# First pass of attention beside HGRN: two 128-query score tiles share one PSUM tile of two banks

## The chip, the cores and the metric

The kernel runs on one core of a Trainium2 chip. The metric is the time of one execution on the device in microseconds (us). A core has a matrix engine (PE; PEld is its weight load, which runs beside it), a vector engine (DVE), an activation engine (ACT), a general engine (POOL) and a queue engine (SP) that issues most of the transfers. Each of them works through its own instructions in order. Matmuls write to PSUM, which has eight banks, each of 512 float32 columns on 128 partitions.

## What is computed

Two layers of a transformer block over 256 context tokens and 2048 latent tokens. One input projection feeds four groups of heads: RG-LRU, HGRN2, a convolution and differential attention. Their gated outputs are joined, projected and added to the stream. The part that matters here is the softmax of attention, whose denominator the kernel finds in a first pass:

```
def attend(q, keys, vals):
    s = jnp.einsum('bqhd,bkhd->bhqk', q, keys).astype(jnp.float32) * scale
    p = jax.nn.softmax(s, axis=-1)
    ...
    a = (p[:, :, 0] - lam * p[:, :, 1]).astype(vals.dtype)
    return jnp.einsum('bhqk,bkhe->bqhe', a, vals)
```

## The kernel before

The instructions are written in one order, and a scheduler of the tile framework, which simulates the engines, decides at build time in which order each engine gets them. On the chip the order on each engine is then fixed.

A layer has four parts. `half0` projects the first half of the tokens. `half1` projects the second half, and beside it run `hgrn` (the HGRN2 scan) and `passes` (the first pass of attention). `first` runs the first 92 of 148 (second layer: 144) steps of the second pass, `attention`, beside `lrus` (two RG-LRU scans), the convolution's norms, `out_weights` (splitting the output weights on POOL) and, in the first layer, `modulations` for the next one. `second` runs the remaining steps beside the output projection and the two convolutions.

`passes` works on one pair of heads `hp` after the other. For each block of 512 queries and each block of keys (256 for block 0, else 512) it calls `pieces`: 16 tiles of 128 queries, each a matmul (score tile `sa`, L1004), a row maximum on DVE (`nm`, L1005), and an Exp with its row sum on ACT (L1006). There are 448 such tiles in each layer. In the code, key blocks 3 and 4 come first, and blocks 0, 1 and 2 last for the queries of the second half: 32 tiles each, those of block 0 only 256 columns wide. `extremes` then turns maxima and sums into one offset per query, transposes it on PE through another `sa` tile, and stores it (`mzd`, L1143).

The PSUM tiles `sa` come from the pool `psA1`: four buffers of one bank. `psm` (`pm`, HGRN) has three banks and `pj1` (`pj`, projections) has one. When `half1` ends, its pools are given up, and those of `first` take their place: `psB` (`sb`, `po`) five banks, `psA2` one, `pq1` two. So an `sb` of the second pass can't be written before `passes` has given up its banks. Before the first `sb`, SP loads the queries (`qst`, L996), the offsets (L1049) and the keys (`kst`, L986).

In a step of `att_b`, PE makes four score matmuls (`sb`, L1176), ACT takes two Exps of 1024 columns (L1180), DVE combines two halves (L1185), and PE adds the step's values to `po` (L1157), some steps later. The first convolution instruction on DVE (L913) that follows in a layer stands, in both kernels, behind the 93rd combination L1185.

Of the kernel before, what the change touches and what calls it, by code (L numbers as in the profile page):

```python
# [8 lines left out]
F32 = mybir.dt.float32  # L9
# [3 lines left out]
AF = mybir.ActivationFunctionType  # L13
ALU = mybir.AluOpType
AX = mybir.AxisListType
# [3 lines left out]
P = 128  # L19
# [35 lines left out]
BLOCKS = [(0, 256)] + [(256 + 512 * j, 512) for j in range(4)]  # L55
# [42 lines left out]
class _Kern:  # L98
# [1000 lines left out]
                yield  # L1099

    def pieces(self, k, c, q, r):
        for s in range(4):
            for i in range(4):
                j = s * 4 + i
                self.piece(k, BLOCKS[c][1], q, s, i, r[0][:, j, c : c + 1], r[1][:, j, c : c + 1])
            yield

    def extremes(self, l, hp, b, nm, zc):

        nc, ap_ = self.nc, self.pc  # L1110
        n = BLOCKS[b][1]
        N = 4 * (n // P)
        C = 5 if b else 1
        with self.tc.high_priority():
            v = nc.vector
            mz = ap_.tile([P, 2, 16], F32, name="mz", bufs=2)
            tm = ap_.tile([P, 16], F32, name="tm", bufs=2)
            if C > 1:
                ng = ap_.tile([P, 16], F32, name="ng", bufs=2)
                v.tensor_reduce(out=ng[:, :N], in_=nm[:, :N, :], axis=AX.X, op=ALU.min)  # L1120
                v.tensor_tensor(
                    out=nm[:, :N, :], in0=ng[:, :N].unsqueeze(2).to_broadcast([P, N, C]), in1=nm[:, :N, :], op=ALU.subtract
                )
                nc.scalar.activation(out=nm[:, :N, :], in_=nm[:, :N, :], func=AF.Exp)
                v.tensor_tensor(out=zc[:, :N, :], in0=zc[:, :N, :], in1=nm[:, :N, :], op=ALU.mult)
                v.tensor_reduce(out=tm[:, :N], in_=zc[:, :N, :], axis=AX.X, op=ALU.add)
                nc.scalar.activation(out=tm[:, :N], in_=tm[:, :N], func=AF.Ln)
            else:
                ng = nm[:, :, 0]
                nc.scalar.activation(out=tm[:, :N], in_=zc[:, :N, 0], func=AF.Ln)  # L1130
            v.tensor_tensor(out=tm[:, :N], in0=tm[:, :N], in1=ng[:, :N], op=ALU.subtract)
            hi = ap_.tile([P, 16], F32R, name="mhi", bufs=2)
            v.tensor_copy(out=hi[:, :N], in_=tm[:, :N])
            v.tensor_copy(out=mz[:, 0, :N], in_=hi[:, :N].bitcast(F32))
            v.tensor_tensor(out=mz[:, 1, :N], in0=tm[:, :N], in1=hi[:, :N].bitcast(F32), op=ALU.subtract)

            mzd = self.dr.tile([2, N, P], F32, name=f"mzd{l}_{hp}_{b}")
            pt = self.psA.tile([P, 512], F32, name="sa")
            for g in range(2):
                nc.tensor.transpose(pt[:N, g * P : (g + 1) * P], mz[:, g, :N], self.ident)  # L1140
            mt = ap_.tile([16, 2, P], F32R, name="mt")
            v.tensor_copy(out=mt[:N].rearrange("n g p -> n (g p)"), in_=pt[:N, : 2 * P])
            nc.sync.dma_start(out=mzd.rearrange("g n p -> n g p"), in_=mt[:N].bitcast(F32))  # L1143
            self.mzd[hp, b] = mzd
# [521 lines left out]
```

## Time and profile before

| what | value |
|---|---|
| three timed runs | 3856.81, 3852.32, 3845.16 us, median 3852.32 |
| the profiled execution | 3839.82 us |
| its span, first to last instruction | 3838.0 us |
| mean granted TensorE clock | 0.943 of full |
| busy: PE, PEld, DVE, ACT, POOL | 90%, 63%, 69%, 58%, 26% |

The profiled execution is 12.5 us below the median of the timed runs. A busy share is a mean over stages that differ; matmuls are pipelined, and the time of one in the profile is its latency, so that the distance between two starts says what one costs in a row of its kind. PEclk is the granted clock, where 1.00 is 2.4 GHz and 0.50 is 1.2 GHz.

### The profile page before, as it was taken

How to read it: one execution, taken by the hardware profiler on the slowest of the kernel's cores; microseconds unless marked ns; L12 is line 12 of the kernel's file. 1: busy time of each engine (PE TensorE's matmuls, PEld its weight loads, DVE VectorE, ACT ScalarE, POOL GpSimd, SP SyncE). 2: the span in 40 equal slices, each digit the busy share in tenths (PEclk: the TensorE clock that was granted, in tenths of full speed). 3: DMA queues.
4: the chain of work that ended last, by engine and by line, in shares of the span. 5: the costliest groups of instructions: out<-in, count | busy, mean ns of one | idle time of the engine just before them, and what ended most of it. 6: DMA issues, size and time to landing. Idle time of an engine off the chain costs nothing. (4 is left out here: it accounts for less than half of the span.)

```text
span 3838.0 us, 61038 instructions
## 1 busy us (share of the span) xinstructions
PE 3471.8 (90%) x21140; PEld 2426.5 (63%) x21140; DVE 2640.7 (69%) x4287; ACT 2211.1 (58%) x4750; POOL 1011.9 (26%) x1588
## 2 busy tenths in 40 slices
PE   6899898999999879999988899889999997899998
PEld 4668676667778634365666686666676784334466
DVE  5967746777787376697438777467887763768842
ACT  3164644766787468755421646536777874886621
POOL 2412124443452130001114231154534203100010
PEclk9899998998999989999999899889999998899999
DMA  5645446434333663443346545364443237434133
GB/s 217 218 163 162 145 165 171 140 114 125 116 96 101 179 221 111 144 131 109 132 142 202 174 168 170 133 177 136 143 125 104 90 102 202 151 89 162 61 124 107
DMA packets 390444, 549.27 MB, mean 143 GB/s; under 512 B 78376, under 2 KB 232024, under 8 KB 390104
## 3 DMA queue, kind: packets, MB, share of 16 engines
q1 hardware_dynamic: 313320, 438.37, 36.9%
q10 hardware_dynamic: 76816, 107.00, 8.0%
q8 instruction: 168, 2.75, 0.3%
q14 instruction: 140, 1.15, 0.1%
HBM read 349.68 MB, written 195.56 MB: 142 GB/s over the span
## 5 line engine op out<-in xcount | busy, mean ns | idle before, releaser
L1006 ACT ACTIVATE sa<-sa,nm 128x512 f32<-128x512 f32 (+1 forms) x1296 | 795.8, 614 | 492.7 <-DVE nm L1005 476.8
L1005 DVE TENSOR_REDUCE nm<-sa 128x1 f32<-128x512 f32 (+1 forms) x1296 | 787.9, 628 | 353.0 <-PE sa L1004 347.7
L499 PE MATMUL pj<-h,wh 128*128 128x256 f32 (+1 forms) x3712 | 962.1, 346 | 39.5 <-ACT s L557 15.2
L499 PEld LDWEIGHTS pj<-h,wh 128*128 128x128 f32 x3712 | 656.7, 197 | 140.0 <-issue 17.4
L1180 ACT ACTIVATE pb<-sb 128x1024 f32<-128x1024 f32 x584 | 568.9, 1019 | 204.3 <-PE sb L1176 192.3
L499 PE MATMUL pj<-h,wl 128*128 128x256 f32 (+1 forms) x1856 | 635.5, 342 | 2.1 <-DMA wl<-wp 2.1
L1185 DVE SCALAR_TENSOR_TENSOR pb<-pb,lam 128x1024 f32<-128x1024 f32 x292 | 381.2, 1307 | 225.0 <-ACT pb L1180 220.4
L1176 PE MATMUL sb<-qst,kst 98*128 98x512 f32 (+1 forms) x1168 | 402.9, 454 | 58.9 <-ACT pb L1180 46.6
L1176 PEld LDWEIGHTS sb<-qst,kst 98*128 98x128 f32 x1168 | 196.0, 198 | 322.8 <-ACT pb L1180 254.8
L499 PEld LDWEIGHTS pj<-h,wl 128*128 128x128 f32 x1856 | 364.2, 196 | 44.3 <-DMA wl<-wp 2.9
L1004 PE MATMUL sa<-k,q 96*128 96x512 f32 (+1 forms) x896 | 351.8, 433 | 31.6 <-ACT sa L1006 29.5
L913 DVE SCALAR_TENSOR_TENSOR m<-m,cols 128x1280 f32<-128x1280 f32 (+1 forms) x240 | 373.9, 1567 | 5.5 <-ACT m L908 4.9
L1157 PE MATMUL po<-pb,V 128*64 128x512 f32 (+1 forms) x1168 | 327.1, 641 | 11.3 <-DVE pb L1185 10.7
L499 PE MATMUL pj<-hx,wh 128*128 128x512 f32 x896 | 297.9, 405 | 10.9 <-ACT s L557 9.6
L1006 ACT ACTIVATION_READ_ACCUMULATOR sa<-sa,nm 128x1 f32 x1296 | 257.7, 199 | 0.6
L133 POOL TENSOR_SCALAR wh<-w 128x1024 fp32r<-128x1024 f32 x56 | 70.4, 1258 | 627.9 <-PE pj L499 521.6
L1004 PEld LDWEIGHTS sa<-k,q 96*128 96x128 f32 x896 | 161.6, 191 | 99.3 <-ACT sa L1006 59.5
L499 PEld LDWEIGHTS pj<-hx,wh 128*128 128x128 f32 x896 | 168.4, 192 | 49.4 <-ACT s L557 10.4
L148 POOL TENSOR_SCALAR rsq<-rsq 128x8 f32<-128x8 f32 (+2 forms) x45 | 16.2, 360 | 659.3 <-DVE rsq L1221 658.5
L133 POOL TENSOR_SCALAR mq<-Q 64x256 f32<-64x256 f32 x238 | 107.7, 454 | 282.0 <-PE pm L1464 170.6
L1004 PE MATMUL sa<-h,xs 96*128 96x512 f32 (+1 forms) x384 | 155.0, 419 | 28.2 <-ACT sa L1006 27.9
L499 PE MATMUL pj<-hx,wl 128*128 128x512 f32 x448 | 179.7, 401 | 0.0
(287 smaller groups left out, 5592.3 us busy)
## 6 DMA issues: line engine op xcount, KB each, us to landing
w<-in_w_in_dram SPq DMA_DIRECT2D x56, 512.0 KB
wp<-wh SPq DMA_DIRECT2D x56, 512.0 KB
wp<-wl SPq DMA_DIRECT2D x56, 512.0 KB
wh<-wp SPq DMA_DIRECT2D x56, 512.0 KB
wl<-wp SPq DMA_DIRECT2D x56, 512.0 KB
ctab<-in_rope_dram SPq DMA_DIRECT2D x32, 512.0 KB
wmod<-in_w_mod_dram SPq DMA_DIRECT2D x32, 512.0 KB
wo<-wop SPq DMA_DIRECT2D x32, 512.0 KB
```

What stands on the lines that cost most here:

```text
L133: self.nc.gpsimd.tensor_scalar(out=out, in0=in_, scalar1=1.0, scalar2=1.0, op0=ALU.mult, op1=ALU.mult)
L148: gp.tensor_scalar(out=ss, in0=ss, scalar1=scale, scalar2=eps, op0=ALU.mult, op1=ALU.add)
L499: nc.tensor.matmul(ps[:, :n], a[:, k, :], hT[:, part, k, o : o + n], start=(m == 0), stop=(m == 23))
L913: nc.vector.scalar_tensor_tensor(out=acc[:, :W], in0=vb[:, k : k + W], scalar=self.col(l, C_FW + 2 * k + ct), in1=acc[:, :W], op0=ALU.mult ...
L1004: nc.tensor.matmul(ps[:, :kn], qst[s][:96, q * P : (q + 1) * P], kst[:96, s, :], start=True, stop=True)
L1005: nc.vector.tensor_reduce(out=nm, in_=ps[:, :kn], axis=AX.X, op=ALU.max, negate=True)
L1006: nc.scalar.activation(out=ps[:, :kn], in_=ps[:, :kn], func=AF.Exp, bias=nm, accum_out=zc)
L1157: nc.tensor.matmul(po[64 * h : 64 * h + 64, :n], V[:, ki, 64 * h : 64 * h + 64], cbs[h][:, :n], start=(kt == 0), stop=(kt == nk - 1), skip ...
L1176: qk = nc.tensor.matmul(ps[:, m, :n], kst[:98, 2 * h + m, ki * P : (ki + 1) * P], qst[2 * h + m][:98, :n], start=True, stop=True,)
L1180: self.exp = nc.scalar.activation(out=pb[:, h, :, :n], in_=ps[:, :, :n], func=AF.Exp)
L1185: nc.vector.scalar_tensor_tensor(out=pb[:, :, 1, :n], in0=pb[:, :, 1, :n], scalar=self.pr["nlam"], in1=pb[:, :, 0, :n], op0=ALU.mult, op1= ...
```

## The change

`pieces` takes two tiles of queries at a time: one PSUM tile of two banks (two buffers in place of four), two matmuls one after the other, then two maxima, then two Exps. Nothing else changes in what is computed; the number and the shapes of instructions are the same. `extremes` takes the same kind of tile and uses its first bank. `early`, the part of the first pass in `half0`, still uses `piece`.

```
     def pieces(self, k, c, q, r):
+
+        nc, n = self.nc, BLOCKS[c][1]
         for s in range(4):
-            for i in range(4):
+            for i in (0, 2):
+                ps = self.psA.tile([P, 2, 512], F32, name="sa", bufs=2)
                 j = s * 4 + i
-                self.piece(k, BLOCKS[c][1], q, s, i, r[0][:, j, c : c + 1], r[1][:, j, c : c + 1])
+                for h in range(2):
+                    nc.tensor.matmul(
+                        ps[:, h, :n], q[s][:96, (i + h) * P : (i + h + 1) * P], k[:96, s, :], start=True, stop=True
+                    )
+                for h in range(2):
+                    nm = r[0][:, j + h, c : c + 1]
+                    nc.vector.tensor_reduce(out=nm, in_=ps[:, h, :n], axis=AX.X, op=ALU.max, negate=True)
+                for h in range(2):
+                    nc.scalar.activation(
+                        out=ps[:, h, :n], in_=ps[:, h, :n], func=AF.Exp, bias=r[0][:, j + h, c : c + 1],
+                        accum_out=r[1][:, j + h, c : c + 1],
+                    )
             yield
...
-            pt = self.psA.tile([P, 512], F32, name="sa")
+            pt = self.psA.tile([P, 2, 512], F32, name="sa", bufs=2)[:, 0]
```

The scheduler orders the whole program anew. (In the changed kernel the matmul is at L1109, and lines behind L1120 are 14 higher: `sb` L1190, `po` L1171, `mzd` L1157.)

On PE in the middle of the first layer's pass, before the change, a single tile (`sa`) stands between runs of HGRN matmuls (`pm`):

```order
L1004 MATMUL sa<-k_10062,q_9289 128x256
L1369 MATMUL pm<-Vb,kt 64x64 x4
L1383 MATMUL pm<-Sn,Vb 64x128 x2
L1004 MATMUL sa<-k_10062,q_9289 128x256
L1388 MATMUL pm<-Q,Sf 64x128 x2
L1004 MATMUL sa<-k_10062,q_9289 128x256
L1383 MATMUL pm<-Sn,Vb 64x128 x2
```

Now, in the same layer, it is pairs:

```order
L1383 MATMUL pm<-Vb,kt 64x64 x4
L1397 MATMUL pm<-Sn,Vb 64x128 x2
L1402 MATMUL pm<-Q,Sf 64x128 x2
L1397 MATMUL pm<-Sn,Vb 64x128 x2
L1478 MATMUL pm<-mq_5104,mk 32x64 x3
L1109 MATMUL sa<-k_8357,q_8365 128x512 x2
L1478 MATMUL pm<-mq_5104,mk 32x64 x5
```

Counted over the pass, an `sa` matmul is directly followed by a `pm` 191 times in the first layer and 160 times in the second before, 97 and 88 times now.

On PE at the end of the second layer's pass, before, the last score tiles (`q_26792` is the last block of queries) stand among the projections (`pj<-h`); 216 more projection matmuls follow behind them, and the first `sb` stands among those:

```order
L1004 MATMUL sa<-k_27917,q_26792 128x512 x2
L1140 MATMUL sa<-ident,mz 16x128 x2
L499 MATMUL pj<-h_22107,wh 128x256 x2
L499 MATMUL pj<-h_22107,wl 128x256
L499 MATMUL pj<-h_22107,wh 128x256 x2
```

Now the last projection comes first. Behind it follow 100 score tiles (96 in the first layer) together with the RG-LRU's gates (`pj<-m,lw`) and the norms (`pj<-m,ones`):

```order
L499 MATMUL pj<-h_22205,wl 128x256
L1109 MATMUL sa<-k_25378,q_26408 128x512 x4
L1109 MATMUL sa<-k_26771,q_26064 128x256 x8
L833 MATMUL pj<-m,lw 128x512 x2
L1109 MATMUL sa<-k_26771,q_26064 128x256 x4
L833 MATMUL pj<-m,lw 128x512 x2
L1109 MATMUL sa<-k_26771,q_26064 128x256 x2
L833 MATMUL pj<-m,lw 128x1
```

At its end, the pass alone is left, and the second pass begins behind it:

```order
L1109 MATMUL sa<-k_27104,q_26408 128x512 x2
L1109 MATMUL sa<-k_27485,q_26064 128x512 x16
L1109 MATMUL sa<-k_27485,q_26408 128x512 x16
L1154 MATMUL sa<-ident,mz 16x128 x4
L1190 MATMUL sb<-qst,kst_30553 128x512 x14
L1171 MATMUL po<-pb,V_30558 64x512 x2
L1190 MATMUL sb<-qst,kst_30553 128x512 x2
```

In the first layer the 144 matmuls of `modulations` have moved in the same way: before they stood among the second pass, now they all stand among the last score tiles.

On SP at that place in the second layer, before, the stores of the offsets follow weight loads (`wh`, `wl`), and the queries of the second pass follow them:

```order
L483 DMA wh<-wp_7_1_20177 128x1024
L484 DMA wl<-wp_7_1_20177 128x1024
L1143 DMA mzd_1_3_28265<-mt 16x2x128
L1143 DMA mzd_1_4_28334<-mt 16x2x128
L996 DMA qst<-qh_18343 32x512
L996 DMA qst<-ql_18344 32x512
```

Now the loads of the RG-LRU (`m<-...`) and of the output weights (`wo<-`, stored again as `wo<-wop` when POOL has split them) come before these, and the last keys of the pass (`k_27485`) stand between them:

```order
L1509 DMA wo_30703<-wop 128x2x512
L1505 DMA wo<-in_w_out_dram 128x512
L986 DMA k_27485<-kh_18121 32x4x512 x2
L986 DMA k_27485<-kl_18122 32x4x512
L865 DMA m<-g_1_18114 128x1023
```

The queries stand behind the offsets, at the end of these:

```order
L899 DMA m<-lyf_18128 128x1023
L865 DMA m<-g_1_18114 128x1023
L1157 DMA mzd_1_3_27817<-mt 16x2x128
L1157 DMA mzd_1_4_27886<-mt 16x2x128
L996 DMA qst<-qh_18119 32x512
```

What moved: the last fifth of the pass now stands behind the projections, the work that used to accompany the first 92 steps of the second pass stands beside that fifth, and the second pass follows both.

## Rows read from the trace of the kernel before

**Rows 1.** Busy time by stage (window, its length, each engine's us; PEclk, DMA share)

```profile
620.00:1266.00 646.00, 606.79 (x5488) 460.50 (x5488) 502.38 (x1146) 455.24 (x1298) 269.10 (x578) 0.95 0.41 123
1266.00:1313.00 47.00, 36.69 (x270) 33.78 (x270) 3.99 (x15) 5.74 (x13) 1.91 (x5) 0.96 0.76 176
1313.00:1613.00 300.00, 260.74 (x1237) 113.04 (x1238) 199.28 (x219) 230.97 (x266) 58.43 (x51) 0.93 0.50 153
1506.00:1606.00 100.00, 99.34 (x398) 38.50 (x396) 58.30 (x49) 84.76 (x91) 6.01 (x5) 1.00 0.28 74
3162.00:3195.00 33.00, 26.93 (x205) 24.71 (x203) 2.77 (x10) 5.34 (x11) 0.91 (x3) 1.00 0.70 170
3195.00:3482.00 287.00, 253.05 (x937) 105.30 (x938) 186.72 (x161) 231.08 (x261) 55.55 (x47) 0.92 0.44 137
```

**Rows 2.** The Exps of the second pass (L1180, ACT) in three of these windows

```profile
1313.00:1613.00 300.00, 185.80 (x192) 0.93 0.50 153
1506.00:1606.00 100.00, 83.09 (x87) 1.00 0.28 74
3195.00:3482.00 287.00, 187.56 (x192) 0.92 0.44 137
```

**Rows 3.** The combinations of the second pass (L1185, DVE) in two windows

```profile
1313.00:1613.00 300.00, 121.24 (x93) 0.93 0.50 153
3195.00:3482.00 287.00, 124.73 (x93) 0.92 0.44 137
```

**Rows 4.** PE in order of time, in the pass (start us, us, instruction)

```profile
1054.56 0.28 PE L499 MATMUL pj<-h,wl 128*128 128x256 f32 x1
1054.68 0.40 PE L1004 MATMUL sa<-k,q 96*128 96x512 f32 x1
1054.91 0.40 PE L499 MATMUL pj<-h,wh 128*128 128x256 f32 x2
...
1055.59 0.63 PE L1464 MATMUL pm<-mq,mk 128*32 128x64 f32 x26
1056.15 0.50 PE L1004 MATMUL sa<-k,q 96*128 96x512 f32 x1
1056.58 0.42 PE L1464 MATMUL pm<-mq,mk 128*32 128x64 f32 x12
1056.93 0.51 PE L1004 MATMUL sa<-k,q 96*128 96x512 f32 x1
```

**Rows 5.** Longest waits of PE in the first layer's pass, then in the second's

```profile
PE sa L1004 <- ACT sa L1006: 13.0, 25, 1.8
...
PE sa L1004 <- ACT sa L1006: 16.5, 33, 1.3
```

**Rows 6.** Row maxima (DVE) and Exps (ACT) back to back, and the mean narrow maximum

```profile
1262.21 2.49 DVE L1005 TENSOR_REDUCE nm<-sa 128x1 f32<-128x512 f32 x4 [2.33 <-PE sa L1004]
...
1260.61 0.66 ACT L1006 ACTIVATE sa<-sa,nm 128x512 f32<-128x512 f32 x1
1261.18 0.21 ACT L1006 ACTIVATION_READ_ACCUMULATOR sa<-sa,nm 128x1 f32 x1
1261.27 0.67 ACT L1006 ACTIVATE sa<-sa,nm 128x512 f32<-128x512 f32 x1
...
L1005 DVE TENSOR_REDUCE nm<-sa 128x1 f32<-128x256 f32 x32 | 12.9, 421 | 12.0 <-PE sa L1004 11.5
```

**Rows 7.** End of the first layer's pass: last tiles, SP's issues, first `sb`

```profile
1261.78 1.09 PE L1004 MATMUL sa<-k,q 96*128 96x512 f32 x4
...
1266.32 4.92 SPq L1143 DMA_DIRECT2D mzd<-mt  x2
1271.33 0.37 SPq L996 DMA_DIRECT2D qst<-qh  x1
...
1280.21 0.38 SPq L978 DMA_DIRECT2D V<-av  x1
...
1284.96 0.70 PE L1176 MATMUL sb<-qst,kst 98*128 98x512 f32 x2 [0.61 <-DMA V<-av]
```

**Rows 8.** SP's stores of split output weights, two of sixteen, four stores apart

```profile
1326.19 0.38 SPq L1495 DMA_DIRECT2D wo<-wop  x1
...
1339.75 0.38 SPq L1495 DMA_DIRECT2D wo<-wop  x1
```

## Prediction

> **What bounds the kernel now.** I read the busy times by stage first, then PE's instructions in the pass in order of time, then the waits, and last the handover from the pass to the second pass. The windows [rows 1] show different limits. In the first layer's pass (620 to 1266) PE is busy 607 of 646 us, DVE 502 and ACT 455; with starts back to back [rows 4], PE sets the pace there. Then come 47 us (second layer 33) of projections alone: the last score tile starts at 1261.78 [rows 7] and DVE and ACT have next to nothing. Then come the first 92 steps of the second pass, 300 and 287 us, with the RG-LRU, the norms and (first layer) the modulations beside them. There PE is busy 261 of 300 and 253 of 287, ACT 231 and 231, DVE 199 and 187: no engine is full. Once that company is gone (1506 to 1606) PE is at 99.3 of 100 us at a granted clock of 1.00, and 87 Exps go by [rows 1, 2].
>
> **The change part by part.** The numbers of matmuls, maxima and Exps stay, so the time can change only by order and by waits. I sum four parts for each layer (first / second), against the profiled execution of 3839.8 us (span 3838.0).
>
> a) Until the last projection. The order now has 96 / 100 score tiles behind the last projection, where it had none. A score matmul of 512 columns between projections takes 0.23 us to the next start (1054.68 to 1054.91), a projection of 256 takes 0.12 [rows 4]. The first layer moves 64 wide and 32 narrow tiles out: 64 x 0.23 + 32 x 0.12 = 19; the second 68 wide, 32 narrow: 19.5. Second, PE changes between score and HGRN matmuls less often: 191 to 97, and 160 to 88. A score matmul ahead of HGRN matmuls takes 0.43 (1056.15 to 1056.58) in place of 0.23, and the runs of 26 and 12 HGRN matmuls take 0.56 and 0.35 us, which is 0.015 for each and 0.17 for the run [rows 4]. So one change costs about 0.20 + 0.17 = 0.37 us: 94 x 0.37 = 35, 72 x 0.37 = 27. Third, the window of projections alone has 270 and 205 matmuls [rows 1]; at 0.12 that is 32 and 25 us, and it takes 47 and 33. Those projections now have score pairs among them; of these 15 and 8 us I count about half, 8 and 5. Sum 62 / 51. The 0.37 comes from one place, and a pair can make PE wait where a single did not, so I take some 85%: **53 / 43** us earlier. Bounds: the moved tiles alone (19), or all.
>
> b) From the last projection to the last score tile, a new stretch. DVE has the most to do in it. Four wide maxima back to back take 2.49 us, so 0.62 each; a narrow one has a mean of 0.42 [rows 6]. 64 x 0.62 + 32 x 0.42 = 53; second layer 56. The other DVE work that accompanied the 92 steps comes into it: what DVE did there less the combinations, 199 - 121 = 78 and 187 - 125 = 62 [rows 1, 3]. Floor: 131 / 118. (About 9 us of it may stay behind as norms of later heads, so 122 / 109 is the lowest I allow.) ACT has less: Exps start 0.66 us apart (1260.61, 1261.27) [rows 6], so 96 and 100 of them take at most 63 and 66 us, and the other work that it had beside the second pass is 231 - 186 = 45 and 231 - 188 = 43 [rows 1, 2]: 108 / 109. PE's matmuls fit below both. How full DVE gets no row shows, since the maxima depend on matmuls, the Exps on maxima, a PSUM tile comes free only after two Exps, and the gates go to and fro between DVE, ACT, PE and SP. The nearest rows are the same gates beside the old 92 steps, where the busiest engine was filled to 87% and 88% [rows 1]. I take that: 131 / 0.87 = **150**, 118 / 0.88 = **135**. Upper bound: DVE is filled no better than it was there, 66% and 65%: 198 / 182.
>
> c) From the last score tile to the first `sb`. Before, it took from 1262.7 (the last of four matmuls at 1261.78) to 1284.96: the sums are finished, SP issues two offset stores at 1266.32, which hold it for 4.9 us, then the queries, the keys and the values, the last of which releases the `sb` [rows 7]. Then, projections covered it. Now SP has the same sequence behind the last tile, and nothing of weight is left on PE, so it is exposed: **20** each. If keys and values are loaded ahead, some 10 are left. Queued behind these stores are the loads of all 92 steps, and PE, ACT and DVE wait for those.
>
> d) The 92 steps without company. A step has two Exps, so 87 in 100 us [rows 2] are 43.5 steps, 2.30 us each: 92 x 2.30 = **211**, in place of 300 / 287. This is the best supported term: it is the same loop at a full PE. The granted clock was 0.93 and 0.92 in the old windows and 1.00 in that stretch [rows 1]. Were it as in the old windows, a step would take 2.30 / 0.93 and the term 227.
>
> The sum: first layer -53 + 150 + 20 + 211 - 300 = +28; second -43 + 135 + 20 + 211 - 287 = +36. Together **+64 us**: 3904 on the profiled scale. The median of the timed runs is 12.5 above the profiled execution, so 3852 + 64, about **3915**. Behind the 93rd combination both kernels have one order, so I carry the shift to the end unchanged.
>
> One edit at nothing: the last keys of the second layer's pass stand on SP behind 11 of the 16 stores of split weights. Those stores went out 3.4 us apart (13.56 for four) [rows 8], so 11 need some 38 us from POOL's first; the first two thirds of the tail cover that. Without the cover (POOL begins late) the last 32 tiles come up to 38 us late, in the second layer only.
>
> On a) a rule speaks against the saving. [rows 1] show PE busy for 607 of 646 us, and its weight load for 460, which is 71%. The Trainium skill's page "Perfetto Trace Analysis", section "Identifying the Most-Contended Engine", says that the busy share of matmuls is a poor measure of a full PE, and that the weight load's share is a better one. By that, PE has slack in the pass and fewer changes save nothing; only the moved tiles would, and the sum would be about +121. The starts in [rows 4] stand back to back, so I keep PE as the pace there.
>
> **The rivals.**
>
> Faster. The maxima of a pair come before its Exps, and a single's matmul waited for an Exp in both layers: 13.0 and 16.5 us [rows 5]. If pairs remove these too, if a) comes in full (62 + 51), and if DVE is nearly full in the tail (122 + 109), the sum is -113 - 29 + 231 + 40 + 422 - 587 = -36, so about 3816. For it: the work is independent enough that a scheduler could fill DVE. Against it: no stage of the old kernel fills DVE above 78%. With the other terms as taken, it decides at two tails of 221 us together: -96 + 221 + 40 + 422 - 587 = 0, and that is less than their floors of 131 + 118. So faster needs a larger a) as well.
>
> Pairs stall PE in the pass. Before, four tiles were each given back after their own Exp. Now there are two, given back after the second Exp, and a tile whose first Exp is done waits for another 0.66 us [rows 6]. For 176 pairs ahead of the last projection this is up to 116 us a layer if nothing covers it; about half, 58 for each layer, would give 3915 + 116 = about 4030. For it: PE is the pace there, and HGRN matmuls queue behind a waiting `sa`. Against it: PE waited 13 and 16.5 us in all for Exps of the pass, in 25 and 33 waits [rows 5], so buffers were seldom short. The Trainium skill, "Perfetto Trace Analysis", section "Matmuls", asks for independent matmuls to rotate through banks, so that one is read out while the next is written; two tiles of two banks still do so, in coarser steps.
>
> No measurable change. With a) in full, tails of 238 us together give a sum of nothing, 3852: that is 7 above the lowest floors, and as unlikely as a DVE filled to the last.
>
> **How the numbers follow.** The forecast's mechanism .58, the faster case .15, stalls in the pass .12, no change .09, other slow ways (SP's queue delays the keys, a lower clock behind a thin tail) .06. About 0.3% (12 us) is what a measurement of this kernel can tell from none. Faster .15, same .09, slower .76. The range: its low end takes the tails at their lowest (122 + 109, so -54), a) in full (-17) and half of the waits (-15): 3915 - 86 = 3829. The tails at 198 + 182 give +95, 4010; that both reach this bound is the extreme, so I leave its last 15 us out with the stalls' case: 3995.
>
> **What would show it.** First layer: the last projection stands near 1260 in place of 1313; behind it comes a stretch of about 150 us in which DVE is the busiest engine at 85 to 90% and PE is well below; then some 20 us without PE, then `sb` at 2.3 us a step with PE at 99%; the first convolution instruction (L913 before, at 1613) comes 28 us later, and the second layer's (3482 before) 64 later. If `sa` in the pass shows waits for Exps much beyond 13 and 16.5 us, stalls are the cause. If DVE is filled to two thirds in the tail, the upper end holds. I am wrong altogether if the second pass starts before the last score tiles, or if steps without company don't run at 2.3 us from the first on.

## The result and the profile after

The changed kernel takes 3950.89 us (median of four runs, 3945.97 to 3959.28); the kernel before takes 3848.74 us (four runs, 3833.49 to 3856.81). The ratio on record is 1.029, with a 95% interval of 1.0265 to 1.0316, and the two medians alone give 1.0265: slower by 102 us between the medians, where 64 were forecast, inside the range given. The profiled executions lie further apart, 3957.5 against 3838.0 us of span (119.5), since the profiled one after is the longest of its four and the one before lies below its median. The stages below are those of the profiled executions.

The windows of the changed kernel answer to [rows 1]; the columns are the same:

```profile
620.00:1251.60 631.60, 580.23 (x5656) 456.02 (x5655) 455.57 (x1045) 403.10 (x1105) 273.30 (x585) 0.96 0.42 127
1251.60:1411.40 159.80, 102.22 (x445) 58.00 (x447) 118.67 (x202) 112.96 (x261) 41.02 (x38) 0.59 0.66 213
1411.40:1431.40 20.00, 4.62 (x42) 2.84 (x42) 4.70 (x21) 4.94 (x10) 0.00 (x0) 0.50 0.51 125
1431.40:1451.40 20.00, 19.30 (x50) 7.88 (x50) 7.71 (x6) 13.65 (x15) 0.00 (x0) 0.66 0.99 190
...
1491.40:1511.40 20.00, 19.20 (x67) 7.77 (x68) 10.87 (x12) 13.95 (x15) 1.21 (x2) 0.83 0.08 27
...
1564.30:1664.30 100.00, 96.81 (x392) 38.39 (x391) 56.46 (x50) 82.73 (x91) 7.81 (x7) 1.00 0.34 88
1431.40:1664.30 232.90, 222.71 (x862) 88.54 (x862) 125.63 (x110) 185.30 (x201) 14.11 (x13) 0.95 0.29 72
...
3201.60:3354.40 152.80, 77.59 (x177) 38.95 (x176) 113.22 (x158) 113.90 (x266) 38.60 (x36) 0.60 0.50 164
3354.40:3374.50 20.10, 1.18 (x4) 0.25 (x5) 3.48 (x12) 4.79 (x10) 0.00 (x0) 0.50 0.43 101
3374.50:3394.50 20.00, 19.34 (x40) 8.24 (x42) 6.42 (x5) 11.60 (x12) 0.00 (x0) 0.51 1.03 195
...
3374.50:3600.90 226.40, 223.05 (x865) 88.02 (x865) 126.70 (x108) 187.16 (x199) 14.20 (x11) 0.96 0.30 74
```

The new stretch behind the last projection (1251.6 to 1411.4, and 3201.6 to 3354.4) is there, and in it no engine is full: in the first layer DVE 119 of 160 us (74%), ACT 113 (71%), PE 102 at a granted clock of 0.59; in the second DVE 113 of 153 (74%), ACT 114, PE 78 at 0.60. The 92 steps behind the gap run with PE at 96 and 99%, but not from their first 20 us on, where the clock is 0.66 and 0.51.

The table gives the stages of all kernels of this study whose stages are spoken of, in us, first layer / second. Each is a difference of starts: from the pass's first score tile to the last projection; from there to the last score tile (the tail); from there to the first `sb` (the gap); from there to the first L913 (the steps). Where the tail is missing, the steps are counted from the last projection.

| kernel | pass to last projection | tail | gap | steps | sum against before |
|---|---|---|---|---|---|
| before | 657.7 / 629.0 | none | none | 300.6 / 287.9 | |
| changed | 596.3 / 587.6 | 159.1 / 152.3 | 20.7 / 20.8 | 232.9 / 226.4 | +50.7 / +70.2 |
| interleaved | 601.4 / 603.2 | 278.6 / 282.9 | 20.4 / 20.3 | 227.8 / 225.6 | +169.9 / +215.1 |
| banks3 | 627.6 / 624.4 | 108.1 / 120.9 | 27.6 / 29.4 | 243.5 / 226.5 | +48.5 / +84.3 |
| late20 | 577.0 / 566.3 | 94.1 / 103.9 | 28.2 / 35.3 | 248.2 / 224.7 | -10.8 / +13.3 |
| swap | 602.9 / 598.8 | 94.7 / 89.3 | 21.3 / 21.4 | 280.0 / 266.6 | +40.6 / +59.2 |
| pcswap | 639.8 / 596.4 | 139.1 / 152.7 | 11.6 / 7.5 | 232.7 / 226.5 | +64.9 / +66.2 |
| warmfill | 598.2 / 603.2 | 159.2 / 148.4 | 24.5 / 21.7 | 227.4 / 224.6 | +51.0 / +81.0 |
| warmfill2 | 594.2 / 606.0 | 157.0 / 150.3 | 37.6 / 36.6 | 227.6 / 220.9 | +58.1 / +96.9 |
| weight200 | 587.0 / 599.9 | 166.1 / 149.8 | 20.9 / 20.7 | 230.1 / 223.2 | +45.7 / +76.7 |
| late20pc | 591.0 / 587.9 | 104.3 / 88.8 | 16.0 / 10.6 | 247.5 / 238.1 | +0.4 / +8.4 |
| late30pc | 600.8 / 590.2 | 83.2 / 80.0 | 20.8 / 11.5 | 248.1 / 239.8 | -5.5 / +4.6 |

What paces the tail is seen where the pass is alone, at its end in the second layer. All engines of the changed kernel in order of time (start, us, engine and instruction; in brackets the idle time before it and its releaser); it answers to [rows 6]:

```profile
3346.19 1.22 PE L1109 MATMUL sa<-k,q 96*128 96x512 f32 x2 [0.26 <-ACT sa L1116]
3347.29 0.66 ACT L1116 ACTIVATE sa<-sa,nm 128x512 f32<-128x512 f32 x1 [1.16 <-DVE nm L1114]
3347.45 1.29 DVE L1114 TENSOR_REDUCE nm<-sa 128x1 f32<-128x512 f32 x2 [0.19 <-PE sa L1109]
...
3348.10 0.66 ACT L1116 ACTIVATE sa<-sa,nm 128x512 f32<-128x512 f32 x1
...
3348.78 0.65 ACT L1116 ACTIVATE sa<-sa,nm 128x512 f32<-128x512 f32 x1
3348.93 1.22 PE L1109 MATMUL sa<-k,q 96*128 96x512 f32 x2 [1.52 <-ACT sa L1116]
...
3349.58 0.66 ACT L1116 ACTIVATE sa<-sa,nm 128x512 f32<-128x512 f32 x1
...
3350.41 1.22 PE L1109 MATMUL sa<-k,q 96*128 96x512 f32 x2 [0.26 <-ACT sa L1116]
```

Follow one tile pair. Its matmuls start at 3346.19 and take 1.22 us. Its first maximum starts at 3347.45, when both matmuls are done. Its first Exp starts at 3348.78, when both maxima are done (3347.45 + 1.29 = 3348.74). The next pair's matmuls into the same banks start at 3350.41, when both Exps are done. So the pair goes from engine to engine as one unit, once round in 4.22 us, and only two units are under way (the other one's matmuls start at 3348.93): four tiles in 4.22 us, 1.055 us each, with DVE at work for 2.58 us of each round and ACT idle for 1.16. In the kernel before, Exps stood 0.66 us apart [rows 6].

Part of the round is the clock's. The granted clock from 3346.1 to 3350.4 is 0.50, and a pair's two matmuls take 1.22 us; before, at the end of the pass, four took 1.09 [rows 7], which leaves 0.63 for two at 0.23 from start to start [rows 4]. So some 0.6 of the 4.22 us is the low clock (an estimate); no run keeps the clock up there. Where the gates stand beside the tiles, a unit can be held for longer. The longest wait in the second layer's tail, 8.9 us up to a pair's matmuls at 3309.70, ends with an Exp at 3308.88, and ahead of this Exp ACT worked on the gates, with two ACT_TABLE_LOAD instructions of 1.28 us each at 3303.41 and 3305.78. Each tail of the changed kernel has 11 of these (14.1 us of ACT).

The waits of PE for Exps of the pass in the changed kernel (us in total, times, longest): in the first layer's pass, then the second's, which answer to [rows 5], then in the first layer's tail, and the second's:

```profile
PE sa L1109 <- ACT sa L1116: 8.3, 11, 1.8
...
PE sa L1109 <- ACT sa L1116: 7.3, 8, 2.5
...
PE sa L1109 <- ACT sa L1116: 34.3, 23, 4.7
...
PE sa L1109 <- ACT sa L1116: 64.7, 34, 8.9
```

Ahead of the last projection they are shorter than before (13.0 and 16.5); they sit in the tail.

### The profile page after: what moved, and what is told of

Its sections match the earlier page's. It is cut to its first block, busy times and chain, and to the rows that moved or that the text cites. A ratio compares the mean times of both kernels' runs of the same rounds, so it can differ in the third digit from the quotient of the medians.

```text
span 3957.5 us, 60348 instructions
## 1 busy us (share of the span) xinstructions
PE 3480.0 (88%) x21140; PEld 2423.1 (61%) x21140; DVE 2644.2 (67%) x4287; ACT 2239.1 (57%) x4750; POOL 1007.9 (25%) x1588
## 4 chain that ended last, share of the span: by engine, by line
PE 63%; DVE 10%; DMA 9%; ACT 6%; issue 3%; POOL 3%; SPq 2%; ACTq 0%; POOLq 0%; DVEq 0%
PE pj L499 27%; PE sb L1190 7%; PE po L1171 6%; PE sb L1564 5%; PE pout L1564 4%; PE sa L1109 3%; DVE nm L1114 2%; DVE m L913 2%; ACT sa L1116 2%; PE sa L1004 2%; DMA wmod<-in_w_mod_dram 1%; SPq L996 1%; PE pm L1478 1%; DMA Kk<-hkb 1%; PE pj L833 1%
## 5 line engine op out<-in xcount | busy, mean ns | idle before, releaser
L499 PEld LDWEIGHTS pj<-h,wh 128*128 128x128 f32 x3712 | 647.9, 196 | 151.3 <-DVE s L517 23.5
L1114 DVE TENSOR_REDUCE nm<-sa 128x1 f32<-128x512 f32 (+1 forms) x896 | 538.4, 645 | 203.9 <-PE sa L1109 202.7
L1199 DVE SCALAR_TENSOR_TENSOR pb<-pb,lam 128x1024 f32<-128x1024 f32 x292 | 372.9, 1277 | 249.4 <-ACT pb L1194 248.9
L1109 PE MATMUL sa<-k,q 96*128 96x512 f32 (+1 forms) x896 | 330.4, 459 | 116.1 <-ACT sa L1116 114.7
L1190 PE MATMUL sb<-qst,kst 98*128 98x512 f32 (+1 forms) x1168 | 388.2, 446 | 39.2 <-DMA V<-av 27.5
L1190 PEld LDWEIGHTS sb<-qst,kst 98*128 98x128 f32 x1168 | 191.4, 196 | 317.9 <-ACT pb L1194 259.4
L913 DVE SCALAR_TENSOR_TENSOR m<-m,cols 128x1280 f32<-128x1280 f32 (+1 forms) x240 | 373.1, 1564 | 6.3 <-ACT m L908 5.5
L1005 DVE TENSOR_REDUCE nm<-sa 128x1 f32<-128x512 f32 (+1 forms) x400 | 230.3, 589 | 185.9 <-PE sa L1004 184.8
L1171 PE MATMUL po<-pb,V 128*64 128x512 f32 (+1 forms) x1168 | 323.8, 635 | 10.2 <-DVE pb L1199 7.1
L499 PE MATMUL pj<-hx,wh 128*128 128x512 f32 x896 | 296.6, 404 | 11.5 <-ACT s L557 10.2
L1109 PEld LDWEIGHTS sa<-k,q 96*128 96x128 f32 x896 | 157.0, 212 | 186.1 <-ACT sa L1116 157.8
L1116 ACT ACTIVATION_READ_ACCUMULATOR sa<-sa,nm 128x1 f32 x896 | 176.7, 197 | 0.5
```

The source lines that it names most:

```text
L499: nc.tensor.matmul(ps[:, :n], a[:, k, :], hT[:, part, k, o : o + n], start=(m == 0), stop=(m == 23))
L913: nc.vector.scalar_tensor_tensor(out=acc[:, :W], in0=vb[:, k : k + W], scalar=self.col(l, C_FW + 2 * k + ct), in1=acc[:, :W], op0=ALU.mult ...
L1005: nc.vector.tensor_reduce(out=nm, in_=ps[:, :kn], axis=AX.X, op=ALU.max, negate=True)
L1109: nc.tensor.matmul(ps[:, h, :n], q[s][:96, (i + h) * P : (i + h + 1) * P], k[:96, s, :], start=True, stop=True)
L1114: nc.vector.tensor_reduce(out=nm, in_=ps[:, h, :n], axis=AX.X, op=ALU.max, negate=True)
L1116: nc.scalar.activation(out=ps[:, h, :n], in_=ps[:, h, :n], func=AF.Exp, bias=r[0][:, j + h, c : c + 1], accum_out=r[1][:, j + h, c : c + 1],)
```

## The experiments

Four theories were tested. Theory 1: the shared tile is a unit that is waited for and given back as a whole, and two such units are too few; this both makes the pass fall behind and paces its tail. Theory 2: it is the grouping in the code. Theory 3: it is the gates, norms and modulations that moved ahead of the second pass. Theory 4: it is the new order as such. All ratios are against the kernel before on the same chip.

**onebank.** The pair's code with four tiles of one bank (the edits below are shown in part):

```
-                ps = self.psA.tile([P, 2, 512], F32, name="sa", bufs=2)
+                ps = [self.psA.tile([P, 512], F32, name="sa") for h in range(2)]
...
-                        ps[:, h, :n], q[s][:96, (i + h) * P : (i + h + 1) * P], k[:96, s, :], start=True, stop=True
+                        ps[h][:, :n], q[s][:96, (i + h) * P : (i + h + 1) * P], k[:96, s, :], start=True, stop=True
...
```

> The pair's code order (two matmuls, two maxima, two Exps), but each score tile in a PSUM tile of its own, four buffers of one bank. The scheduler gives every engine the same instructions in the same order as in the kernel before. Theory 1 (the shared tile is the cause: it is waited for and given back as a whole, so two units are alive where there were four) expects the time of the kernel before, ratio 1.000 within 0.003. Theory 2 (the grouping in the code is the cause, two of a kind in a row) expects most of the 1.029.

Measured 0.9995 (0.9977 to 1.0014). Two matmuls, two maxima and two Exps in a row in the code change nothing. Theory 2 falls; the 1.029 hangs on the shared tile alone, with the order that the scheduler makes of it.

**interleaved.** The shared tile, with each half taken through before the next: the two inner loops over `h` ahead of the maxima and the Exps go.

```
                 for h in range(2):
+                    nm = r[0][:, j + h, c : c + 1]
                     nc.tensor.matmul(
                         ps[:, h, :n], q[s][:96, (i + h) * P : (i + h + 1) * P], k[:96, s, :], start=True, stop=True
                     )
-                for h in range(2):
-                    nm = r[0][:, j + h, c : c + 1]
                     nc.vector.tensor_reduce(out=nm, in_=ps[:, h, :n], axis=AX.X, op=ALU.max, negate=True)
-                for h in range(2):
                     nc.scalar.activation(
```

> The shared tile of two banks, two buffers, but in the code each half goes through matmul, maximum and Exp before the next half starts. In the order built, 181 and 191 score tiles stand behind the last projection (96 and 100 in the changed kernel). Theory 1: the second half's matmul then waits for the first half's Exp, since the tile is waited for as a whole, so only two score tiles are ever under way; each further tile behind the projections costs about 1.05 us (the changed kernel's last lone pairs: 4.22 us for four tiles), the end of the projections comes some 70 us earlier in each layer, and the sum is about 270 us over the kernel before, ratio 1.05 to 1.09. Theory 2 (grouping in the code) expects the time of the kernel before. Theory 3 (the loss is the gates, norms and modulations that moved out of the 92 steps, whatever the score tiles do) expects about the changed kernel's 1.029 or less, since the same work has moved.

Measured 1.0952 (1.0917 to 1.0987), above the range of theory 1 and far from the others. At the end of the tail of its second layer, the engines in order of time:

```profile
3601.82 0.79 PE L1110 MATMUL sa<-k,q 96*128 96x512 f32 x1 [0.45 <-ACT sa L1114]
3602.14 0.66 ACT L1114 ACTIVATE sa<-sa,nm 128x512 f32<-128x512 f32 x1 [0.37 <-DVE nm L1113]
3602.65 0.69 DVE L1113 TENSOR_REDUCE nm<-sa 128x1 f32<-128x512 f32 x1 [0.55 <-PE sa L1110]
...
3602.97 0.79 PE L1110 MATMUL sa<-k,q 96*128 96x512 f32 x1 [0.35 <-ACT sa L1114]
...
3603.38 0.66 ACT L1114 ACTIVATE sa<-sa,nm 128x512 f32<-128x512 f32 x1 [0.46 <-DVE nm L1113]
...
3604.21 0.79 PE L1110 MATMUL sa<-k,q 96*128 96x512 f32 x1 [0.45 <-ACT sa L1114]
```

A matmul at 3601.82, its maximum at 3602.65, its Exp at 3603.38, and the next matmul in that tile at 3604.21: two tiles in 2.39 us. Each shared tile holds one live half, so half of the four banks are idle, and two tiles are under way, as with two buffers of one bank (a kernel with two such buffers was not run). A tile costs 1.2 us here and not the 1.05 that I had put in, which is why the tails are 280 us. That is about half of the miss: the projections also ended only 56 and 26 us earlier, and not 70.

**banks3.** The kernel before with three buffers (`"psA1", 4` becomes `"psA1", 3`).

> The kernel before with three buffers of one bank for the score tiles in place of four. In the order built, 69 and 79 score tiles stand behind the last projection, with the same gates and norms and part of the modulations among them. Theory 1: the stretch behind the projections takes about 60 and 49 us for its other work (the changed kernel's 160 and 153 less 1.04 for each tile) and 0.75 for each tile, so some 112 and 108 us; with 35 and 29 us saved ahead of it, about 65 us over the kernel before, ratio 1.012 to 1.022. Theory 3 (the moved work) expects 1.027 or more, since nearly all of it has moved here too and less is saved ahead.

Measured 1.0277 (1.0254 to 1.03): a miss, it is theory 3's number. The windows of its two tails:

```profile
1276.50:1384.60 108.10, 71.57 (x222) 36.66 (x220) 83.90 (x126) 77.65 (x179) 37.56 (x38) 0.64 0.66 219
...
3224.20:3345.10 120.90, 74.04 (x158) 36.07 (x156) 94.24 (x130) 95.48 (x217) 40.50 (x36) 0.62 0.57 192
```

The tails, 108 and 121 us, came near the expected 112 and missed the 108. What was wrong is the rest: 30 and 5 us saved ahead of the last projection in place of 35 and 29, gaps of 28 and 29 in place of 20, and 243 us of steps in the first layer. Its loss is thus made up otherwise than the changed kernel's. This run alone does not decide between theories 1 and 3.

**late20.** Four buffers of one bank, with an order near that of the changed kernel forced by a smaller weight:

```
-        mix([[self.hgrn(l), 100], [self.passes(l), 100], ...
+        mix([[self.hgrn(l), 100], [self.passes(l), 20], ...
```

> The kernel before, four buffers of one bank, but the first pass has a weight of 20 in place of 100 beside HGRN and the projections, so that 77 and 85 score tiles stand behind the last projection, with the gates, the norms and part of the modulations, as in the changed kernel; changes from a score tile to HGRN are 88 and 80 (changed kernel 97 and 88). It has the order of the changed kernel without its shared tiles. Theory 1: a tile alone takes 0.66 us here, the pace of the Exps, so the stretch behind the projections takes about 60 + 77 x 0.66 = 111 and 49 + 85 x 0.66 = 105 us; the projections end some 60 and 44 us earlier; the sum is about 23 us over the kernel before, ratio 1.003 to 1.010. Theory 4 (the order alone makes the loss, not the unit) expects the stretch as long as the changed kernel's, less the tiles that are missing: about 145 and 140 us, so some 75 over, ratio 1.02.

Measured 0.9998 (0.998 to 1.0016), less than the 1.003 to 1.010 of theory 1 and far from theory 4's 1.02. Its tails, gaps and steps:

```profile
1233.70:1327.80 94.10, 67.03 (x200) 34.48 (x198) 84.18 (x127) 74.34 (x185) 37.76 (x38) 0.62 0.75 252
1327.80:1356.00 28.20, 19.71 (x84) 9.75 (x83) 14.20 (x34) 24.29 (x38) 0.00 (x0) 0.68 0.38 94
1356.00:1604.20 248.20, 234.91 (x1043) 97.62 (x1044) 142.78 (x155) 190.81 (x208) 15.26 (x13) 0.93 0.38 103
3117.90:3221.80 103.90, 71.53 (x160) 36.35 (x158) 85.64 (x126) 85.34 (x211) 40.77 (x36) 0.66 0.60 199
3221.80:3257.10 35.30, 2.72 (x11) 1.23 (x10) 21.97 (x29) 19.08 (x30) 0.00 (x0) 0.52 0.50 156
3257.10:3481.80 224.70, 220.77 (x865) 86.73 (x865) 126.69 (x108) 187.25 (x199) 15.61 (x11) 0.97 0.30 76
```

77 and 85 score tiles stand behind the projections, with gates, norms and part of the modulations, and the kernel loses nothing: the projections end 81 and 63 us earlier, and the tails take 94 and 104 us, with DVE at 89 and 82% (84.18 of 94.10, 85.64 of 103.90). The changed kernel's tails are 65 and 48 us longer. Not all of that is the unit's: its order is near this one, but not the same. It has 19 and 15 tiles more behind the projections, while here about half of the RG-LRU's work on DVE is still to come when the last score tile starts. It stands in the gap (DVE 14.2 and 22.0 us, in the changed kernel 4.7 and 3.5) and in the first layer's steps. From the last projection to the first `sb` the changed kernel takes 57 and 34 us more. Theory 4 falls in the main, since tiles, gates and norms behind the projections and a second pass without company are here too and cost nothing; so does theory 3 as the main cause. What the two orders still differ in, no run takes apart.

**swap.** The changed kernel with `psm` taken from PSUM before `psA1`.

> The changed kernel with the PSUM pools of the pass and of HGRN taken in the other order. The gates, norms and modulations then stand beside the 92 steps again, as in the kernel before, while 98 and 92 score tiles stand alone between the last projection and the second pass. Theory 1 (units of two tiles, waited for as a whole, set the pace): 1.055 us for each wide tile, some 0.9 for a narrow one, so 98 and 92 us alone; with -61 and -44 us ahead, 20 us of loads and the old 300 and 288 us behind, 57 + 68 = 125 us over the kernel before, ratio 1.033, no better than the changed kernel. Theory 3 (the moved work makes the stretch long): alone, the tiles go at the pace of the Exps, 0.66 us each, so 63 and 60 us, and the sum is about 58 us, ratio 1.015.

Measured 1.0267 (1.0225 to 1.0309). The tails, in which the score tiles now stand alone, and the steps:

```profile
1248.20:1342.90 94.70, 51.18 (x100) 23.97 (x99) 57.66 (x107) 69.62 (x200) 30.63 (x32) 0.53 0.55 172
1364.20:1644.20 280.00, 255.68 (x1216) 110.56 (x1216) 178.58 (x208) 219.36 (x251) 18.14 (x17) 0.94 0.44 123
3194.60:3283.90 89.30, 47.59 (x95) 22.10 (x93) 55.58 (x101) 64.74 (x184) 31.01 (x33) 0.53 0.51 167
3305.30:3571.90 266.60, 247.19 (x925) 102.23 (x926) 171.05 (x152) 223.20 (x248) 16.02 (x14) 0.92 0.35 99
```

98 and 92 tiles alone take 94.7 and 89.3 us (98 and 92 expected by the pace of units, 63 and 60 by that of the Exps), with DVE at 61 and 62%. Without the moved work the tails are 64 and 63 us shorter, and the steps 47 and 40 us longer. So its place made at most 17 and 23 us of the changed kernel's loss, and in the second layer 8 tiles fewer in the tail are some 8 of the 23. Since the projections end 7 and 11 us later, the table's sums differ by 10 and 11 us only. The bare tails, at the pace of the units, make the most of the loss. Theory 1 said 1.033, above the interval; the steps were 20 us shorter than I had put in, each layer.

**weight200.** The changed kernel with `[self.passes(l), 200]`.

> The changed kernel with a weight of 200 in place of 100 for the pass beside HGRN and the projections, so that its tiles come earlier in the order in which the code is written. In the order built, 100 and 94 score tiles still stand behind the last projection (96 and 100 in the changed kernel). Theory 1 (two units limit how fast the pass can go): 1.029, within 0.004. If it were a matter of priority, more weight would bring back at least half of the loss: 1.015 or less.

Measured 1.031 (1.0271 to 1.035), as theory 1 said: more weight leaves as many tiles behind the projections, and the loss stays.

**banks5.** Five buffers for the pass and two for `psm`.

> The kernel before with five buffers of one bank for the score tiles and two for HGRN (four and three before). In the order built the last score tile stands 543 and 555 projection matmuls ahead of the last projection (288 and 216 before). Theory 1: with four, nothing of the pass is exposed any more, so a fifth buys nothing: 1.000 to 1.010, the excess being HGRN's missing bank and more projections alone. If each further unit went on paying as the step from two to three (1.095 to 1.028) and from three to four (to 1.000) did, it would be 0.985 to 0.995.

Measured 1.0001 (0.9981 to 1.0022). The fifth bank is taken from HGRN here, so that the run shows both together. With two, three, four and five units of one bank the ratios are 1.095 (interleaved, which has two under way), 1.028, 1 and 1.000: four are enough, and a fifth at HGRN's expense buys nothing. Two units of two banks give 1.029.

**pcswap.** The changed kernel with the SBUF pool `hg` taken before `pc`.

> The changed kernel with its two SBUF pools of the pass taken in the other order, so that the queries and keys of the second pass lie where HGRN's tiles were and not where the first pass's tiles are, and can be loaded before the pass ends; 90 and 100 score tiles stand behind the last projection. If the 20.0 and 20.1 us between the last score tile and the first score matmul of the second pass (1411 to 1431, 3354 to 3375) are the loads queued on SP behind the last offsets, as I predicted, most of them vanish: 30 to 40 us under the changed kernel, ratio 1.019 to 1.021. If they are PSUM banks or the extremes themselves, the ratio stays at 1.029.

Measured 1.0338 (1.029 to 1.0386), not the ratio expected. PE at the end of its second layer's pass:

```profile
3377.07 1.22 PE L1109 MATMUL sa<-k,q 96*128 96x512 f32 x2 [1.53 <-ACT sa L1116]
3378.55 0.59 PE L1154 MATMUL sa<-ident,mz 128*16 128x128 f32 x2 [0.26 <-ACT sa L1116]
3384.11 0.58 PE L1154 MATMUL sa<-ident,mz 128*16 128x128 f32 x2 [4.97 <-DVE mz L1149]
3385.20 2.07 PE L1190 MATMUL sb<-qst,kst 98*128 98x512 f32 x4 [0.51 <-DVE mt L1156]
```

The first `sb` follows the last transpose at once: the gap falls from 20.7 and 20.8 to 11.6 and 7.5 us, so the gap was loads. But the scheduler orders the first layer's pass otherwise too, and its last projection comes 43 us later, with the tail only 20 shorter. The gap's cause is shown; that removing it pays is not.

**late20pc and late30pc.** Four buffers of one bank, weights 20 and 30, and the pools as in pcswap.

> The kernel before with the pass's weight at 20 and the two SBUF pools in the other order; 85 and 68 score tiles stand behind the last projection, in four buffers of one bank. It took 28 and 35 us there from the last score tile to the first score matmul of the second pass with the weight alone. If these are exposed loads, some 45 to 55 us go: ratio 0.986 to 0.989. If the work queued beside them has to be done anyway, it returns in the 92 steps and the ratio stays at 1.000, within 0.003.

> The kernel before with the pass's weight at 30 and the two SBUF pools in the other order: 61 and 62 score tiles in four buffers of one bank behind the last projection, with part of the gates and modulations. With weight 20 the projections ended 79 and 63 us earlier, and 94 + 28 and 104 + 35 us went by to the second pass. Some 20 tiles fewer at 0.66 us and a gap of 10 to 16 us (as with the same pools at weight 20) would make 25 to 35 us less in each layer, if the projections still end 60 us earlier: ratio 0.985 to 0.995. If what is taken out of one stretch returns in the next, as at weight 20, 1.000 within 0.003.

Measured 1.0001 (0.9981 to 1.0021) and 1.0003 (0.9978 to 1.0027); neither beats the kernel before. With weight 20 the gaps fell from 28.2 and 35.3 to 16.0 and 10.6 us, while the projections ended 14 and 22 us later and the second layer's steps took 238.0 us in place of 224.7. What left one stretch came back in another in these runs; why the sum stays is not shown. No kernel of the study beats the kernel before.

**warmfill and warmfill2.** The changed kernel with matmuls on PE in the gap whose results nobody reads, in `extremes` behind the transposes (warmfill2 has 125 in place of 32):

```
+            if hp == 1 and b > 2:
+                wm = self.psA.tile([P, 2, 512], F32, name="sa", bufs=2)[:, 0]
+                for _ in range((12, 32)[b - 3]):
+                    nc.tensor.matmul(wm[:, :P], self.ident, self.ident, start=True, stop=True)
```

> The changed kernel with 12 and 32 matmuls of 128x128 more on PE, whose results nobody reads, behind the last two transposes of each layer's pass, so that PE works while it waits for the loads; the order around them stays in the first layer, and nearly in the second. The first 20 us of the second pass ran at a granted clock of 0.66 and 0.51. If PE's idle time ahead of them is why, the clock is up sooner and 7 and 10 us go: ratio 1.024 to 1.026, and a step takes 2.3 us from nearly the start. If not, 1.029, with the same clock in these 20 us.

Measured 1.0337 (1.0301 to 1.0374), neither of the two that were expected: the second layer's projections ended 16 us later than in the changed kernel. The clock of the first 20 us was 0.66 and 0.60. The first layer's gap in finer windows, then two windows of its steps:

```profile
1418.00:1422.00 4.00, 4.00 (x39) 3.98 (x38) 0.72 (x4) 0.00 (x0) 0.00 (x0) 1.00 0.05 12
...
1430.00:1434.00 4.00, 0.00 (x0) 0.00 (x0) 0.00 (x0) 0.00 (x0) 0.00 (x0) 0.62 1.11 225
1434.00:1438.00 4.00, 3.40 (x7) 2.11 (x8) 0.46 (x1) 2.04 (x3) 0.00 (x0) 0.50 1.12 214
...
1434.30:1454.30 20.00, 19.32 (x50) 7.88 (x50) 7.71 (x6) 13.57 (x14) 0.00 (x0) 0.66 0.95 185
...
1494.30:1514.30 20.00, 20.00 (x82) 7.96 (x80) 12.27 (x12) 16.83 (x19) 1.21 (x2) 1.00 0.08 27
```

The clock rose while the idle matmuls ran, and was down again when the second pass began, behind a PE that had gone idle once more.

> As the run with 12 and 32 idle matmuls, but 12 and 125: there the granted clock rose to 1.00 while they ran, then PE stood idle for 8 us more and the clock was back at 0.50 when the second pass began. 125 matmuls at the 0.115 us that they took at the full clock last some 14 us, up to the first score matmul. If PE's idleness just ahead sets the clock, the first 20 us of the second pass now run at 0.9 to 1.0 (0.66 and 0.51 in the changed kernel), the stretch from the first score matmul to the first convolution instruction falls by 5 to 10 us in each layer from 232.9 and 226.4, and in the first layer, where the order ahead is unchanged, that is the whole change. If the transfers that flow then set it, the clock stays as it was.

Measured 1.04 (1.0355 to 1.0444). Each of these matmuls is two on PE, so the 125 ran past the loads and the gap grew to 37.6 and 36.6 us; I had mis-sized the filler. The second layer's projections also ended 18 us later. But the first 20 us of the steps show the clock that was asked for:

```profile
1439.30:1459.30 20.00, 18.79 (x60) 7.03 (x60) 9.90 (x8) 16.47 (x17) 0.00 (x0) 0.91 0.38 69
...
3404.20:3424.20 20.00, 18.59 (x62) 7.10 (x61) 9.53 (x8) 16.01 (x17) 0.00 (x0) 0.91 0.37 82
```

The steps fell from 232.9 and 226.4 to 227.6 and 220.9. In the second layer these 5 us go with the clock: ACT did 16.0 us of work in the first 20 us, in the changed kernel 11.6, and a stretch at 1.00 does 17.6 in 20, so that the difference is worth some 5 us (an estimate). In the first layer the same sum gives 3 us (16.5 against 13.7), and warmfill, whose first 20 us were as slow as the changed kernel's, took 227.4 all the same. So the 5 us there are not shown to be the clock's. What else differs is a second fall of the clock in the changed kernel, to 0.83 in the window from 1491.4, where warmfill has 1.00.

## Why the prediction was right, and where its sizes were off

The sign and the mechanism were right: the pass falls behind, its last fifth is exposed behind the projections with the work that used to accompany the second pass, and the second pass then runs alone. Term by term, forecast and measured, first / second layer:

a) The projections end earlier: 53 / 43 forecast, 61 / 41 measured. PE was the pace in the pass. late20 says so most clearly: it moves 77 and 85 tiles out, which cost PE some 16 and 17 us at [rows 4] (64 wide and 13 and 21 narrow), and saves 81 and 63; its changes from score tiles to HGRN fell to 88 and 80. The changed kernel says it too: from the pass's first score tile to the last projection PE's busy time fell from 617 and 589 us to 555 and 546, as much as the stretch itself, while its idle time stayed at 40 to 42. The price of 0.37 us for a change is thereby not proved: banks3, where the trace counts 153 and 141 changes (195 and 162 before), saved 30 and 5, and the first layer of pcswap, with 90 tiles moved out and 102 changes, saved 18. The weight load's share of 71%, by which the Trainium skill ("Perfetto Trace Analysis", section "Identifying the Most-Contended Engine") would see slack here, was not a sign of slack in this stage: PE stood idle for 41 us of it by the profile, and 81 came out of it in late20 with only 77 score matmuls less.

b) The tail: 150 / 135 forecast, 159 / 152 measured. This term was mis-sized, by more than its total shows. I filled DVE to 87 and 88%; it was at 74%. At my fill, the 119 and 113 us that DVE had to do would have taken 136 and 129, so the fill was 23 us off in each layer; that I had put in 131 and 118 us of work made up for some of it, which was luck. (118 / 0.88 is 134, not 135.) DVE was not the busiest engine in the second layer either: ACT had 113.9 us, DVE 113.2. For tiles of one bank the fill was nearer: late20's tails have DVE at 89 and 82%. I had named that a tile comes free only after two Exps, and had not priced it: two units that go round in 4.22 us, 1.055 us for each wide tile. swap shows this price alone: its bare tails are 32 and 29 us longer than 63 and 60 at the pace of the Exps. Against late20 the result is much the same (an estimate): of 57 and 34 us more from the last projection to the first `sb`, the tiles more are at most 13 and 10 at that pace, and the work that late20 leaves to its first layer's steps, 248.2 us in place of 232.9, is 15; some 30 and 24 are left. In both, the low clock of the tails is in the price. The Trainium skill says of such gaps ("Perfetto Trace Analysis", section "Optimization Strategy") that a bubble that repeats on the engine that should be saturated can mean too few buffers; the trace agrees, with 1.16 us of ACT idle in each round and PE's 34.3 and 64.7 us of waits for Exps.

c) The gap: 20 each forecast, 20.7 and 20.8 measured, and shown to be loads by pcswap. Its last wait in the changed kernel, which answers to [rows 7]:

```profile
1417.11 0.60 PE L1154 MATMUL sa<-ident,mz 128*16 128x128 f32 x2 [1.32 <-DVE mz L1148]
1431.45 2.04 PE L1190 MATMUL sb<-qst,kst 98*128 98x512 f32 x4 [13.74 <-DMA V<-av]
```

d) The steps: 211 forecast, 232.9 / 226.4 measured; the second term that was mis-sized, and the larger. I had called it the best supported one and had made steps at 2.3 us from the first on a sign of being right; that sign failed in the first 20 us, at a clock of 0.66 and 0.51. The Exps of the second pass (ACT), which answer to [rows 2]:

```profile
1431.40:1664.30 232.90, 179.29 (x188) 0.95 0.29 72
1564.30:1664.30 100.00, 79.08 (x84) 1.00 0.34 88
3374.50:3600.90 226.40, 181.70 (x188) 0.96 0.30 74
```

188 Exps are 94 steps, not 92, since Exps run ahead of the combination that I counted by: 2 x 2.30 = 4.6 us. The low clock at their start is some 3 and 5 us (warmfill2). The remaining 14 and 5 us I put down to the norms at the ends of heads, of which my 100 us had too few: the last 100 us of this stretch in the first layer have 84 Exps, not 87. PE's waits in the steps bear out a part: 5.9 us in the first layer are waits for or in these norms (the longest, 2.8 us, is for ACT at L1216), 2.0 in the second. No run takes the norms away, so the rest stays argued.

Together: a) 7 us more saved than forecast, b) 26 longer, c) 1.5, d) 37 longer, which makes the +121 of the table out of +64 (with roundings of 2). The first L913 came 51 us later, and the second layer's 119, where 28 and 64 were forecast. The medians differ by less, 102. The range held since it was wide: it had room for the tails at a DVE filled to two thirds.

Of the rivals, the stall in the pass did not come (8.3 and 7.3 us of waits), but its mechanism, a unit given back after its second Exp, came in the tail, where PE has less else to do. The faster case failed at its tails: it needed 221 us together, and they were 311. In the second layer's tail the profile puts no wait of PE down to the keys, so no delay by the stores on SP is seen.

## What to carry to other kernels

A tile of several banks is one unit to whoever waits for it, so joining tiles halves the number of units under way without saving an instruction; count the units, and price one round of the chain matmul, maximum, Exp, divided by their number, against the busiest engine's time for a tile. Here the scheduler then moved work, and the stretch behind the projections shows the price, not the place where the tiles were joined. To learn whether an order or a resource costs the time, force the order, as nearly as it can be had, with the old resource, as late20 does, and count what still differs.

## What the runs showed of the hardware that was not expected

The granted clock of PE was at 0.59 and 0.60 in the tails, where PE was busy 64% and 51% of the time, and 0.50 (1.2 GHz) in the gaps. In warmfill, 24 and 64 idle matmuls brought it to 1.00 (2.4 GHz) within the gap, and it was back at 0.50 after PE had stood idle to the gap's end. The loads that fill the DMA engines at that place are not what lowers it: in warmfill2, where PE was kept at work beside them, the last 4 us of the first layer's gap read

```profile
1435.00:1439.00 4.00, 4.00 (x38) 4.00 (x36) 0.00 (x0) 0.00 (x0) 0.00 (x0) 1.00 1.13 205
```

with the clock at 1.00 and a DMA share of 1.13. That half a PSUM tile can't be handed over by itself, as interleaved shows, is how this program was built and not a property of the chip: onebank hands over the same four banks one by one.
